# A planner's numbers are measured anew, and the low part of two weights gets all 128 rows

## The chip, the cores and the metric

The kernel runs on one core of one Trainium2 chip. The metric is the device time of one execution in microseconds (us). Before the change the median of three runs was 1872.74 us (1870.92 to 1876.2).

## The reference

One step of an encoder layer, over 1024 prompt rows and 64 sample rows. The normalised input goes through one input projection; half of its columns feed differential attention (8 heads), half feed an RWKV-7 recurrence (16 heads of 64). Both results are gated and go through one output projection. The change touches the decay and rate weights (`w_up`, `a_up`, 64 rows each) and the order in which all of it is emitted.

```python
proj = rms_norm(x, norm_pre) @ w_in
# A: attention on rotated q, k: two softmaxes per head, w = p0 - lam * p1; rms norm; silu gate
# B: RWKV-7 on the token-shifted columns
decay = exp(-exp(-softplus(-(w0 + tanh(wd) @ w_up)) - 0.5))
a = sigmoid(a0 + ad @ a_up)
kk = kb * k_k; kk = kk / max(norm(kk), 1e-12); kb = kb * (1 + (a - 1) * k_a)
for t in time:                      # per head, state s is 64 x 64
    sa = s @ (-kk_t)
    s = s * decay_t + outer(sa, kk_t * a_t) + outer(v_t, kb_t);  y_t = s @ r_t
y_b = (group_norm(y) * ln_w + ln_b + bonus) * silu(g)
out = concat(y_a, y_b) @ w_out
x + rms_norm(out, norm_post); also k, v, the last state, the last shifted row
```

## The kernel before

**Precision.** A value of 32 bits is split into a high and a low part, and a product is done as three matmuls: high by high, low by high, high by low. In the input projection that is a *triple* L215, L216, L217; eight triples fill one tile of 384, 384 or 320 columns, and three tiles make a *job*, the 128 projected columns of one head or pair of heads. The output projection has its triple at L1145, L1146, L1147, of 512 columns.

**Phase B** (L282) works on units: a pair `p` of heads (0 to 7) and a half `hf` of the prompt, 512 rows, which makes 16, and one unit for the sample, put in at the 16th place of 17. A unit first makes its vectors (decay, rate, `kk`: L490 to L620; the decay and rate weights are applied at L513 and L514, once for the high part and once for the low), then 128 x 128 blocks and the inverse of a triangular block by doubling (L630 to L790), and then runs its *chain* of eight chunks of 64 rows (L800 to L850). A chunk of the chain is: two matmuls on the state, L804 and L809; a copy L818 by VectorE; the matmul L821; two copies L827 and L828; the matmuls L832 and L833; two updates of the state L842. The next chunk needs the state. The chains of the units follow one another, while the next unit is prepared.

**Phase A** (L1164) is attention, by head and by tile of 128 queries: scores L1322 and L1323, a maximum L1332 and the sum of weights by VectorE, exponentials L1348 by ACT, transposes L1381, the product with v L1395, and the norm and gate. It starts when all units are done. Its q and k are read back from DRAM by loads that SP issues (L1206, L1207), and the cast of k is at L1249.

**Fillers.** The stream `filler` (L974) emits the projection's jobs: r, k, v and g of each pair as soon as the tiles of the pair before are free, and in between the heads' aq, ak, av, ag, of which `RESERVE = 6` are held back until the pairs are done. Its products are evacuated by ACT and VectorE (a gate's sum at L939, the rotation at L964 to L966). After the last job and the end of phase B the same stream becomes the output projection (L1040): eight groups, 0 to 3 for the RWKV half and 4 to 7 for the attention heads, each over nine tiles of rows. Groups 0 and 2 are evacuated by a copy of ACT, the others by an add of VectorE, L1156. `finish` (L1117) follows group 7.

**What sets the order.** The order is laid when the kernel is built: the order of emission is the priority by which instructions are scheduled, and on the chip each engine runs its own list in order. `Weave` holds streams (generators), sorted by rank: units by their number, fillers 100. It keeps a virtual clock `now` for PE. The first stream that may go on emits its next instructions; `spend(ns)` says how long PE is busy with them, `op(engine, n)` books an operation of n elements in that engine's queue and returns when its result is there, and `yield d` lets the stream go on d ns later. In between, a stream of lower rank emits. So the fillers stand in the gaps that the clock sees, and the numbers of the planner (latency, rate, fixed cost, which operations are booked at all) decide how many triples stand in a gap.

## Time and profile before

| | before |
|---|---|
| median of 3 runs | 1872.74 us (1870.92 to 1876.2) |
| the profiled execution | 1870.95 us |
| its span (first to last instruction) | 1869.1 us |
| mean granted clock of PE | 0.975 |
| PE busy | 1699.6 us, 91% |
| weight loads (PEld) busy | 1500.6 us, 80% |
| VectorE busy | 1305.8 us, 70% |
| ACT busy | 868.1 us, 46% |
| GpSimd (POOL) busy | 695.4 us, 37% |

PE's busy time counts a matmul from its start to its modelled end, and matmuls overlap; how long one holds up the next is read from the distance of two starts. The time that an engine is not busy in a stretch is its wait there. In a wait list, the name behind the arrow is the instruction that came last.

### The profile page before, as it was taken

How to read it: one execution, taken by the hardware profiler on the slowest of the kernel's cores; microseconds unless marked ns; L12 is line 12 of the kernel's file. 1: busy time of each engine (PE TensorE's matmuls, PEld its weight loads, DVE VectorE, ACT ScalarE, POOL GpSimd, SP SyncE). 2: the span in 40 equal slices, each digit the busy share in tenths (PEclk: the TensorE clock that was granted, in tenths of full speed). 3: DMA queues.
4: the chain of work that ended last, by engine and by line, in shares of the span. 5: the costliest groups of instructions: out<-in, count | busy, mean ns of one | idle time of the engine just before them, and what ended most of it. 6: DMA issues, size and time to landing. Idle time of an engine off the chain costs nothing. (4 is left out here: it accounts for less than half of the span.)

```text
span 1869.1 us, 34871 instructions
## 1 busy us (share of the span) xinstructions
PE 1699.6 (91%) x12930; PEld 1500.6 (80%) x12930; DVE 1305.8 (70%) x2892; ACT 868.1 (46%) x2155; POOL 695.4 (37%) x866
## 2 busy tenths in 40 slices
PE   6999899999998999999999899977899798889995
PEld 5888888888888888888888789877778676777784
DVE  5568777777778787886875766524687667787336
ACT  5534444344344444444443433323566576676323
POOL 4442333233233323323332421212332356554657
PEclk9999999999999999999999999998999899899998
DMA  4110111321122111110101121345555565443325
GB/s 144 49 55 27 50 48 48 80 82 36 39 72 62 51 44 35 52 38 29 57 26 50 57 62 50 106 118 160 153 156 149 165 155 156 121 131 105 116 87 181
DMA packets 204244, 158.85 MB, mean 85 GB/s; under 512 B 44229, under 2 KB 185194, under 8 KB 204074
## 3 DMA queue, kind: packets, MB, share of 16 engines
q1 hardware_dynamic: 169242, 137.33, 25.5%
q10 hardware_dynamic: 34832, 19.30, 4.0%
q8 instruction: 102, 1.67, 0.4%
q14 instruction: 68, 0.56, 0.1%
HBM read 108.67 MB, written 47.34 MB: 83 GB/s over the span
## 5 line engine op out<-in xcount | busy, mean ns | idle before, releaser
L1348 ACT ACTIVATE e<-s,nb 128x512 f32<-128x512 f32 (+4 forms) x208 | 117.3, 569 | 59.3 <-DVE nb L1332 26.1
L1145 PE MATMUL po<-woh,mxh 128*128 128x512 f32 x288 | 120.3, 419 | 7.1 <-DVE part L1156 5.9
L1147 PE MATMUL po<-wol,mxh 128*128 128x512 f32 x288 | 115.9, 402 | 3.9 <-DVE nb L1337 2.5
L1146 PE MATMUL po<-woh,mxl 128*128 128x512 f32 x288 | 115.5, 401 | 4.2 <-POOL mxl L158 4.2
L1332 DVE TENSOR_REDUCE nb<-s 128x1 f32<-128x512 f32 (+4 forms) x208 | 108.0, 529 | 15.9 <-PE s L1323 14.6
L158 POOL TENSOR_TENSOR mxl<-mxr,mxh 128x512 fp32r<-128x512 f32 (+1 forms) x72 | 88.3, 1231 | 74.9 <-ACT mxh L157 61.8
L811 ACT ACTIVATE sd<-suv,dc 64x64 f32<-64x64 f32 x128 | 44.4, 347 | 154.1 <-DVE suv L842 149.4
L1322 PE MATMUL s<-k,qs 128*128 128x512 f32 (+4 forms) x208 | 78.9, 385 | 22.0 <-ACT k L1249 10.0
L1395 PE MATMUL x_o<-vn,wt 128*128 128x128 f32 (+1 forms) x608 | 88.0, 289 | 10.1 <-DVE wt L1385 5.4
L1395 PEld LDWEIGHTS x_o<-vn,wt 128*128 128x128 f32 (+1 forms) x608 | 81.0, 200 | 18.5 <-issue 5.5
L1156 DVE TENSOR_TENSOR part<-po,part 128x512 f32<-128x512 f32 x72 | 49.5, 688 | 55.6 <-PE po L1147 55.5
L842 DVE SCALAR_TENSOR_TENSOR suv<-cbank,dc,sd 64x64 f32<-64x64 f32 x224 | 63.0, 281 | 33.3 <-PE cbank L832 29.2
L832 PE MATMUL cbank<-suv,bkt 128*128 128x128 f32 x256 | 56.9, 304 | 32.0 <-DVE suv L828 32.0
L832 PEld LDWEIGHTS cbank<-suv,bkt 128*128 128x128 f32 x256 | 41.1, 190 | 45.7 <-DVE suv L828 43.4
L215 PE MATMUL pj_v<-hhi,wh_v 128*128 128x384 f32 (+1 forms) x192 | 70.1, 365 | 6.5 <-DVE mg L416 6.1
L1409 POOL TENSOR_SCALAR ms<-ms 128x1 f32<-128x1 f32 x72 | 18.0, 249 | 150.9 <-ACT osq L1407 150.4
L1323 PE MATMUL s<-k,qs 128*128 128x512 f32 (+4 forms) x208 | 71.5, 358 | 2.4 <-POOL k L1252 1.5
L215 PE MATMUL pj_av<-hhi,wh_av 128*128 128x384 f32 (+1 forms) x192 | 70.2, 365 | 3.0 <-DVE fl_g L939 3.0
L157 ACT CAST mxh<-mxr 128x512 fp32r<-128x512 f32 (+1 forms) x72 | 40.7, 567 | 68.7 <-PE po L1147 29.4
L677 POOL TENSOR_TENSOR ltlo<-lt,lt 64x512 f16<-64x512 f32 x32 | 37.7, 1177 | 93.4 <-ACT lt L665 92.2
L1145 PEld LDWEIGHTS po<-woh,mxh 128*128 128x128 f32 x288 | 55.4, 192 | 20.6 <-DVE part L1156 4.4
L215 PE MATMUL pj_k<-hhi,wh_k 128*128 128x384 f32 (+1 forms) x192 | 67.7, 352 | 4.0 <-ACT raw_k L230 4.0
(533 smaller groups left out, 6189.5 us busy)
## 6 DMA issues: line engine op xcount, KB each, us to landing
mxr<-mixB SPq DMA_DIRECT2D x32, 256.0 KB
wor<-in_w_out SPq DMA_DIRECT2D x64, 128.0 KB
qa<-scr_q SPq DMA_DIRECT2D x32, 204.0 KB
ka<-scr_k SPq DMA_DIRECT2D x32, 204.0 KB
scr_q<-fl_q SPq DMA_DIRECT2D x8, 544.0 KB
scr_k<-fl_k SPq DMA_DIRECT2D x8, 544.0 KB
scr_v<-fl_v SPq DMA_DIRECT2D x8, 544.0 KB
scr_g<-fl_g SPq DMA_DIRECT2D x8, 544.0 KB
```

The source lines that it names most:

```text
L158: gtt(lo, raw, hi.bitcast(F32), op=SUB)
L215: mm(ps[:, :n], hi[:, k, :], hhi[i][:, k, :], start=(k == 0), stop=False)
L832: mm(s, bkt[:, c], suv[:, c], start=True, stop=True)
L842: stt(suv[r, c + 1, h, :] if c < 7 and not smp else to[r], s[r, h * CH:(h + 1) * CH], dc[r, c:c + 1], sd[r], op0=MUL, op1=ADD)
L1145: mm(ps, hi[:, q, :], wh, start=(q == 0), stop=False)
L1146: mm(ps, lo[:, q, :], wh, start=False, stop=False)
L1147: mm(ps, hi[:, q, :], wl, start=False, stop=(q == len(ks) - 1))
L1322: mm(s[:, 0:w], lq, k1[c][:, k0 + o_:k0 + o_ + w], start=True, stop=False)
L1323: mm(s[:, 0:w], lq, k2[c][:, k0 + o_:k0 + o_ + w], start=False, stop=True)
L1332: nc.vector.tensor_reduce(nb[:, i_:i_ + 1], s[:, 0:w], axis=AX.X, op=MAX, negate=True)
L1348: act(e[:, o_:o_ + w], s[:, 0:w], AF.Exp, bias=mx, accum_out=sm)
L1395: mm(ops[:, 0:P], wt[0:w, b, :], vn[0:w, vb, :], start=(b == 0), stop=(b == len(kbs) - 1))
```

## The change

It has two parts. The same instructions are issued by each engine in the same number; their order changes, and one operand.

**The planner.** A result is there 210 ns after PE (130 or 100 before) and 60 ns after another engine. An operation costs a rate times its elements plus a fixed part for each instruction, which was 80 ns for all and is now 150, 190 and 90 on VectorE, ACT and GpSimd. `op` takes a number of instructions `k` and an earliest start `at`. `spend` adds 130 or 105 ns where the work changes to matmuls on part of the array or back. The fillers' evacuations, shifts, gates and rotations, which were not booked, are. Many sizes of booked operations and spent times are set anew.

**The low part.** L514 multiplied 64 rows of the low part (rows 0 to 63 for `w_up`, 64 to 127 for `a_up`) by the same 64 rows of the input. Now it multiplies all 128 rows, of which the other half belongs to the low part as it lies in the tile.

```diff
-LA, LAT, W_LD, W_DMA = 130, 100, 11000, 3122
+LAT, OUT, W_LD, W_DMA = 210, 60, 11000, 3122
+LA = LAT
+
+T_IN, T_OUT = 130, 105
...
-RS = 1.0
 RATE = {DVE: 1 / 0.96, ACT: 1 / 1.2, POOL: 2.4}
+FIX = {DVE: 150, ACT: 190, POOL: 90}
...
-    def spend(self, ns):
+    def spend(self, ns, part=False):
+
+        if part != self.part:
+            self.part = part
+            ns += T_IN if part else T_OUT
         self.now += ns
...
-    def op(self, eng, n):
-
-        self.free[eng] = max(self.now, self.free.get(eng, 0.0)) + RS * (RATE[eng] * n + 80)
-        return self.free[eng] - self.now + (LA if b_done[0] else LAT)
+    def op(self, eng, n, k=1, at=0.0):
+
+
+        self.free[eng] = max(self.now + at, self.free.get(eng, 0.0)) + RATE[eng] * n + k * FIX[eng]
+        return self.free[eng] - self.now + OUT
...
             nc.scalar.copy(raw[:, 1 + t0:1 + t0 + n], ps)
+            weave.op(ACT, n, at=LAT)
...
                 act(d, raw[:, t0 + 1:t0 + 1 + n], AF.Copy, scale=omu[:, idx:idx + 1])
+                op_(DVE, n, at=op_(ACT, n + 80))
...
                         stt(d_, d_, 1.0, ps[:, a - t0:b - t0], op0=ADD, op1=MUL)
+                        op_(DVE, b - a, at=op_(ACT, b - a, at=LAT))
...
-                    for j, (x, r) in enumerate(((xw, slice(0, 64)), (xa, slice(64, 128)))):
+                    for j, x in enumerate((xw, xa)):
...
                         mm(o_, t[:, j], x[:, cl], start=True, stop=False)
-                        mm(o_, t[r, 2 + j], x[r, cl], start=False, stop=True)
+                        mm(o_, t[:, 2 + j], x[:, cl], start=False, stop=True)
...
-            op_(DVE, 4100)
+            op_(DVE, 8 * 512, 8)
...
-                spend(1800)
+                spend(1400, True)
...
-                yield done(op_(DVE, 6 * 256 + 400), 2)
+                yield done(op_(DVE, 6 * 256, 6), 2)
...
-            d = op_(DVE, 800)
+            d = op_(DVE, 1400, 3)
...
-                op_(DVE, 110)
+                op_(DVE, 128)
...
-            yield op_(DVE, 1200)
+            yield op_(DVE, 1040, 3)
...
             vtt(yo, yo, gate, op=MUL)
+            op_(DVE, 600)
...
                     stt(st_[:, t0:t0 + n], st_[:, t0:t0 + n], 1.0, ps, op0=ADD, op1=MUL)
+                    op_(DVE, n, at=op_(ACT, n, at=LAT))
...
                 vtt(a, a, b, op=ADD)
+                op_(DVE, 3 * W, 3)
...
-        op_(ACT, n)
-        return op_(POOL, n)
+        return op_(POOL, n, at=op_(ACT, n))
...
-            spend(w / 1.2 + 20)
+            spend(w / 1.1 + 10)
...
-            d = op_(ACT, w + 50)
+            d = op_(ACT, w + 80, 2)
```

The lines move by some: the chain's L804, L821, L832 are L818, L835, L846 after the change, the projection's triple is L224 to L226, the low part L526 and L527, the output projection's triple L1161 to L1163.

Three places show what the order does. The first is PE in a chunk of a chain, between L821 and L832 before. `cbank` is the chain's PSUM tile, `pj_k` a projection tile, `m_bo` a product of the next unit.

```order
L821 MATMUL cbank<-gsb_01_4937,xtf 128x128
L651 MATMUL m_bo_10_4961<-t_kbh_1_4784,bdr 128x512
L652 MATMUL m_bo_10_4961<-t_kbl_1_4785,bdr 128x512
L215 MATMUL pj_k_1_4911<-hhi_174,wh_k_4531 128x384
L216 MATMUL pj_k_1_4911<-hlo_177,wh_k_4531 128x384
L217 MATMUL pj_k_1_4911<-hhi_174,wl_k_4532 128x384
L215 MATMUL pj_k_2_4978<-hhi_175,wh_k_4531 128x320
L832 MATMUL cbank<-suv_0_4717,bkt_0_4689 128x128
L833 MATMUL y_00_4807<-suv_0_4717,rbk_0_4008 128x128
L216 MATMUL pj_k_2_4978<-hlo_178,wh_k_4531 128x320
L217 MATMUL pj_k_2_4978<-hhi_175,wl_k_4532 128x320
```

After the change, such a place between L835 and L846 of the same unit (`y_00`), with the four matmuls of the decay and rate weights (`m_up`) just ahead; `pj_av` is a projection tile. The dots stand for the rows up to the last matmul of the fourth triple.

```order
L526 MATMUL m_up_00_5379<-xw,t_wus_00_5381 128x512
L527 MATMUL m_up_00_5379<-xw,t_wus_00_5381 128x512
L526 MATMUL m_up_01_5380<-xa,t_wus_00_5381 128x512
L527 MATMUL m_up_01_5380<-xa,t_wus_00_5381 128x512
L835 MATMUL cbank<-gsb_01_5372,xtf 128x128
L224 MATMUL pj_av_0_5348<-hhi_173,wh_av_5092 128x384
L225 MATMUL pj_av_0_5348<-hlo_176,wh_av_5092 128x384
L226 MATMUL pj_av_0_5348<-hhi_173,wl_av_5093 128x384
...
L226 MATMUL pj_av_1_5411<-hhi_174,wl_av_5093 128x384
L554 MATMUL m_ss_00_5425<-on_483,t_sq_0_5395 128x2 x4
L846 MATMUL cbank<-suv_0_5109,bkt_0_5047 128x128
L847 MATMUL y_00_5194<-suv_0_5109,rbk_0_4312 128x128
```

Before, two matmuls of a unit, one triple and the first matmul of a second stand in the gap, and the triple goes on behind the chain's L833. After, four triples and a short sum of a unit stand in it, and no triple is cut; the four `m_up` rows read alike in shape.

The second place is PE in the last unit's chain. Before, it is one round of it:

```order
L804 MATMUL cbank<-suv_1_14687,pt_498 128x128
L809 MATMUL y_14_14954<-suv_1_14687,pt_498 128x128
L215 MATMUL pj_ak_0_15011<-hhi_173,wh_ak_14842 128x384
...
L217 MATMUL pj_ak_0_15011<-hhi_173,wl_ak_14843 128x384
L821 MATMUL cbank<-gsb_15_15020,xtf 128x128
L215 MATMUL pj_ak_0_15011<-hhi_173,wh_ak_14842 128x384
...
L217 MATMUL pj_ak_0_15011<-hhi_173,wl_ak_14843 128x384
L832 MATMUL cbank<-suv_1_14687,bkt_1_14656 128x128
L833 MATMUL y_14_14954<-suv_1_14687,rbk_1_14035 128x128
L215 MATMUL pj_ak_0_15011<-hhi_173,wh_ak_14842 128x384
```

After the change, a round and the start of the next:

```order
L835 MATMUL cbank<-gsb_13_16022,xtf 128x128
L846 MATMUL cbank<-suv_1_15879,bkt_1_15848 128x128
L847 MATMUL y_10_15949<-suv_1_15879,rbk_1_15188 128x128
L1161 MATMUL po_16268<-woh_16234,mxh_16218 128x512
L1162 MATMUL po_16268<-woh_16234,mxl_16219 128x512
L1163 MATMUL po_16268<-wol_16235,mxh_16218 128x512
L818 MATMUL cbank<-suv_1_15879,pt_498 128x128
L838 MATMUL y_14_16034<-suv_1_15879,pt_498 128x128
L1161 MATMUL po_16284<-woh_16234,mxh_16224 128x512
L1162 MATMUL po_16284<-woh_16234,mxl_16225 128x512
L835 MATMUL cbank<-gsb_14_16038,xtf 128x128
L1161 MATMUL po_16268<-woh_16248,mxh_16218 128x512
```

Before, two projection triples stand in each of these gaps, of tile `pj_ak`; after, no projection is left, and one to three matmuls of the output projection's first group (`po`) stand in a gap, or none.

The third place is SP's queue where attention's first loads of q (`qa`) are issued. Before:

```order
L928 DMA mixB_124<-ysq_o_1_15216 128x512
L967 DMA rot_q_163<-raq_15167 128x136
L944 DMA scr_k_141<-fl_k_15162 128x1088
L1037 DMA out_shift_p<-sho 25x128
L1037 DMA out_shift_s<-sho 25x128
L949 DMA rot_k_167<-fl_k_15162 16x1088
L950 DMA rot_k_168<-fl_k_15162 8x1088
L1206 DMA qa_15287<-rot_q_160 16x1088
L1207 DMA qa_15287<-scr_q_126 48x1088
```

After the change:

```order
L1098 DMA wor_17520<-in_w_out 128x256
L1116 DMA mxr_16407<-mixB_125 128x4x64
L1054 DMA out_shift_p<-sho 25x128
L1054 DMA out_shift_s<-sho 25x128
L942 DMA mixB_124<-ysq_o_1_16111 128x512
L1116 DMA mxr_16468<-mixB_123 128x4x128
L1116 DMA mxr_16539<-mixB_123 128x4x128
L1222 DMA qa_16162<-rot_q_160 16x1088
L1223 DMA qa_16162<-scr_q_126 48x1088
```

Before, the rotated rows of k (`rot_k`) and the stored projections (`scr_k`) of later heads are still written just ahead of the loads; after, these are gone by then, and loads of rows (`mxr`) and weights (`wor`) for the output projection stand there.

## Rows read from the trace of the kernel before

**Rows 1.** The page, part 1: each engine's busy time, share and instructions.
```profile
PE 1699.6 (91%) x12930; PEld 1500.6 (80%) x12930; DVE 1305.8 (70%) x2892; ACT 868.1 (46%) x2155; POOL 695.4 (37%) x866
```

**Rows 2.** Stretches: length, then PE, PEld, DVE, ACT, POOL busy, clock, DMA.
```profile
0.00:100.00 100.00, 78.04 (x435) 69.25 (x436) 58.29 (x92) 55.04 (x99) 48.07 (x79) 0.95 0.30 93
100.00:1250.60 1150.60, 1090.05 (x9497) 984.48 (x9495) 840.38 (x1820) 472.96 (x1078) 352.28 (x419) 0.99 0.19 54
1250.60:1270.40 19.80, 3.72 (x15) 2.70 (x14) 4.36 (x10) 6.58 (x12) 5.54 (x3) 0.58 0.94 230
1270.40:1746.00 475.60, 423.57 (x2551) 361.61 (x2550) 345.80 (x897) 294.39 (x883) 207.11 (x267) 0.96 0.52 139
1746.00:1870.00 124.00, 104.18 (x441) 82.59 (x439) 57.01 (x74) 39.10 (x85) 82.41 (x99) 0.95 0.43 135
```

**Rows 3.** Waits of PE, 100 to 1250.6: total us, times, longest us.
```profile
PE cbank L832 <- DVE suv L828: 32.0, 36, 3.2
PE cbank L821 <- DVE gsb L818: 7.7, 9, 1.8
...
PE cbank L804 <- DVE suv L842: 2.2, 2, 1.2
```

**Rows 4.** VectorE in order of time around 407 (start us, us, instruction).
```profile
406.75 1.84 DVE L670 TENSOR_TENSOR xt_a<-lt,mt 64x512 f16<-64x512 f16 x2
...
409.91 0.23 DVE L828 COPY suv<-cbank 64x64 f32<-64x64 f32 x1
```

**Rows 5.** PE in order of time around 410.
```profile
410.19 0.49 PE L832 MATMUL cbank<-suv,bkt 128*128 128x128 f32 x2 [0.79 <-DVE suv L828]
410.52 0.39 PE L833 MATMUL y<-suv,rbk 128*128 128x128 f32 x2
410.66 0.39 PE L216 MATMUL pj_k<-hlo,wh_k 128*128 128x320 f32 x1
410.89 0.31 PE L217 MATMUL pj_k<-hhi,wl_k 128*128 128x320 f32 x1
```

**Rows 6.** PE in order of time around 216, the low part.
```profile
215.36 0.30 PE L217 MATMUL pj_aq<-hhi,wl_aq 128*128 128x320 f32 x1
215.50 0.40 PE L513 MATMUL m_up<-xw,t_wus 128*128 128x512 f32 x1
215.83 0.49 PE L514 MATMUL m_up<-xw,t_wus 64*128 64x512 f32 x1
...
217.11 0.49 PE L804 MATMUL cbank<-suv,pt 128*128 128x128 f32 x2
```

**Rows 7.** PE in order of time at 1800, output projection.
```profile
1800.16 0.39 PE L1145 MATMUL po<-woh,mxh 128*128 128x512 f32 x1
1800.39 0.39 PE L1146 MATMUL po<-woh,mxl 128*128 128x512 f32 x1
```

**Rows 8.** PE in order of time at 1014, the sample unit.
```profile
1013.83 0.28 PE L513 MATMUL m_upNone<-xw,t_wusNone 128*128 128x64 f32 x1
...
1017.42 0.44 PE L215 MATMUL pj_av<-hhi,wh_av 128*128 128x384 f32 x1
```

**Rows 9.** PE in order of time, the first score of attention.
```profile
1262.67 0.47 PE L1322 MATMUL s<-k,qs 128*128 128x128 f32 x1 [10.02 <-ACT k L1249]
```

**Rows 10.** VectorE by line, 1262 to 1746: busy us, mean ns.
```profile
L1156 DVE TENSOR_TENSOR part<-po,part 128x512 f32<-128x512 f32 x17 | 11.6, 682 | 3.2 <-PE po L1147 3.1
...
L939 DVE SCALAR_TENSOR_TENSOR fl_g<-fl_g,pj_ag 128x384 f32<-128x384 f32 (+1 forms) x12 | 6.3, 526 | 5.2 <-ACT fl_g L938 5.2
...
L965 DVE TENSOR_TENSOR rbk<-rbk,rtk 128x136 f32<-128x136 f32 x8 | 3.7, 461 | 9.8 <-DMA rbk<-rot_k 6.7 <-DMA rtk<-in_c_rot 3.1
```

**Rows 11.** A stretch of attention (columns as in rows 2).
```profile
1400.00:1450.00 50.00, 48.25 (x330) 45.04 (x329) 39.14 (x111) 33.47 (x102) 15.92 (x25) 1.00 0.55 145
```

**Rows 12.** VectorE, lines L599 and L688: duration ns min/median/max.
```profile
L599 DVE TENSOR_TENSOR pt<-t_kkn,dd x32: 641/689/1766, 76.2 to 1113.4; 64x512 f32<-64x512 f32 x32
...
L688 DVE TENSOR_TENSOR q<-m_ip,mt x80: 664/691/693, 100.9 to 1164.7; 128x512 f16<-128x512 f32 x80
```

More of the change, by code (lines that the diff above doesn't have):

```diff
@@ L70, in __init__ @@
         self.free = {}
+        self.part = False
         self.count = itertools.count()
-    def spend(self, ns):
+    def spend(self, ns, part=False):
+        if part != self.part:
+            self.part = part
+            ns += T_IN if part else T_OUT
         self.now += ns
-    def op(self, eng, n):
-        self.free[eng] = max(self.now, self.free.get(eng, 0.0)) + RS * (RATE[eng] * n + 80)
-        return self.free[eng] - self.now + (LA if b_done[0] else LAT)
+    def op(self, eng, n, k=1, at=0.0):
+        self.free[eng] = max(self.now + at, self.free.get(eng, 0.0)) + RATE[eng] * n + k * FIX[eng]
+        return self.free[eng] - self.now + OUT
     def later(self, ns, call):
@@ L541, in unit @@
                 mm(pss[:, 2 * q:2 * q + 2], sq[:, q * P:(q + 1) * P], on2, start=True, stop=True)
-            spend(1100)
+            spend(900)
             yield LAT
@@ L555, in unit @@
             nc.gpsimd.memset(dd[:, :, 0:1], 1.0)
-            yield op_(DVE, 512)
+            yield op_(DVE, 1020)
             act(dd[:, :, 1:CH + 1], c3(cs), AF.Exp, scale=-C2)
@@ L618, in unit @@
                 stt(kbl, kb, hrk[:, p:p + 1], kbh.bitcast(F32), op0=MUL, op1=SUB)
-            op_(POOL, 960)
-            op_(ACT, 512)
+            if smp:
+                op_(POOL, 512)
+            op_(ACT, 600)
             yield op_(DVE, 512)
@@ L684, in unit @@
                     mm(ps[:, cl], lt16[:, c, :], x_[:, cl], start=True, stop=True)
-                spend(300)
+                spend(240)
                 yield LAT
@@ L694, in unit @@
                         mm(ps[r, cl], q_[r, cl], xt[r, cl], start=True, stop=True)
-                spend(500)
+                spend(340, True)
                 yield LAT
@@ L710, in unit @@
                     mm(ps[r, cl], xt[r, cl], id16[r, :], start=True, stop=True)
-            spend(500)
+            spend(340, True)
             yield LAT
@@ L723, in unit @@
                 mm(ps[:, cl], ltlo[:, c, :], x_[:, cl], start=False, stop=True)
-            spend(600)
+            spend(480)
             yield LAT
@@ L737, in unit @@
                     nc.tensor.transpose(ps[:, c * CH:(c + 1) * CH], src, ident[r, 64 * h:64 * h + 64])
-                spend(500)
+                spend(560, True)
                 yield LAT
@@ L765, in unit @@
                     mm(ps[r, cl], r16[r, cl], xt[r, cl], start=True, stop=True)
-            spend(500)
+            spend(340, True)
             yield LAT
@@ L852, in unit @@
                         nc.scalar.copy(ysb[64:128, 0:CH], y4[64:128, 3, CH:])
-                    op_(ACT, 400)
-                    op_(ACT, 400)
-                yield op_(DVE, 110)
+                    op_(ACT, 570, 3)
+                yield op_(DVE, 128)
             yield lambda: turn["norm"] == n
@@ L873, in unit @@
             gtt(var, var, nh[:, 0:8], op=POW)
-            yield op_(POOL, 700)
+            yield op_(POOL, 800, 2)
             vtt(c3(yc), c3(yc), bcol(var), op=MUL)
@@ L877, in unit @@
             nc.gpsimd.tensor_copy(ycp[64:128, HALF:], ycp[64:128, 0:CH])
-            z_at = weave.now + op_(POOL, 110)
+            z_at = weave.now + op_(POOL, 220)
             if smp or hf == 1:
@@ L939, in evac @@
                     stt(st_[:, t0:t0 + n], st_[:, t0:t0 + n], 1.0, ps, op0=ADD, op1=MUL)
+                    op_(DVE, n, at=op_(ACT, n, at=LAT))
                 else:
                     act(st_[:, t0:t0 + n], ps, AF.Copy, scale=0.125 if kind == "q" else 1.0)
+                    op_(ACT, n, at=LAT)
             yield from proj_cm(w, evac, f"a{kind}{h}")
@@ L1295, in prep @@
                 nc.tensor.transpose(ps[:, t * 64:(t + 1) * 64], k[0:64, t * P:(t + 1) * P], ident[0:64, 0:64])
-            spend(450)
+            spend(450, True)
             yield LA
@@ L1337, in score @@
             vtt(mx, nb[:, 0:1], nb[:, 1:2], op=ALU.min)
-            d = op_(DVE, 60)
+            d = op_(DVE, 10)
         yield d
@@ L1364, in qtile @@
             nc.vector.tensor_reduce(sm, st["sp"], axis=AX.X, op=ADD)
-            op_(DVE, 60)
+            op_(DVE, 10)
         ri = ap_.tile([P, 2], F32, tag="ri", bufs=3, name=f"ri{u}")
@@ L1370, in qtile @@
         stt(w_[:, 0:n], e1[:, 0:n], co, w_[:, 0:n], op0=MUL, op1=ADD)
-        op_(DVE, 400)
-        yield op_(DVE, n)
+        op_(DVE, 130, 2)
+        yield op_(DVE, n + 60)
         yield lambda: (h, 2) in ready
@@ L1403, in qtile @@
         act(on, ops[:, 0:P], AF.Copy, scale=ri[:, 0:1])
-        yield xdone(op_(ACT, P))
+        yield xdone(op_(ACT, 210))
         sq = ap_.tile([P, P], F32, tag="osq", name=f"osq{u}")
@@ L1407, in qtile @@
         act(sq, on, AF.Square, accum_out=ms)
-        yield op_(ACT, P)
+        yield op_(ACT, P, 2)
         gts(ms, ms, 1.0 / P, SUBLN_EPS, op0=MUL, op1=ADD)
```

4 lines of the change are left out of this document (2 added, 2 removed).

## The prediction

> **What bounds the kernel now.** I read the page's first part first. TensorE (PE) is busy for 91% of the span [rows 1], so a change in the order of emission can win only what PE waits, and what PE loses between instructions without being called idle. The second view is the table of stretches [rows 2], where the wait of a stretch is its length less PE's busy time. From 100 to 1250.6 us, in which sixteen prompt units and the sample unit of RWKV run beside the projections, PE waits 1150.6 - 1090.05 = 60.5 us. The passage to attention (1250.6 to 1270.4) holds 3.72 us of PE work in 19.8 us, a wait of 16.1. Attention (1270.4 to 1746) waits 475.6 - 423.57 = 52.0, and the tail 124.0 - 104.18 = 19.8; the first 100 us hold the other 22. The third view, the list of waits of the RWKV stretch, says who is waited for there [rows 3]: 32.0 us go to L832 waiting for the copies of L828, 7.7 to L821 and 2.2 to L804, together 41.9 us on the state chain, which is L804, a copy, L821, two copies, L832, an update, and again. The fourth view shows one such wait close up. VectorE runs a pair of mask products for 1.84 us from 406.75 and other work behind them, so the second chain copy starts only at 409.91 [rows 4]. PE has used up the fillers that were emitted for this gap and stands 0.79 us before L832 at 410.19 [rows 5].
>
> **The low part of the rate weights.** Nothing is removed in count: each prompt unit keeps four 512-column matmuls at L513 and L514 and the sample unit 32 short ones. What goes is the half-array form of L514 (64 rows). The row before them shows a step of 0.14 us between projection matmuls of 320 columns; the four then take from 215.50 to 217.11, 1.61 us [rows 6]. Four 512-column matmuls that keep the full array step by 0.23 us [rows 7], 0.91 us for four. So 0.70 us times 16 units, 11.2 us, on PE's own time and on no other engine. The 32 of the sample unit come in two runs of 16, of which one took 1013.83 to 1017.42, 3.59 us [rows 8], so 7.2 us in all. No row shows such a 64-column matmul in one form: at best the half-array switch is all of it (a gain of 7), at worst it is none. I take 4: by the nearest row, the 320-column step of 0.14, it is 32 x (0.22 - 0.14) = 2.6, and 64 columns are fewer. Sum: **-15**, bounds -11 to -18. The extra low-by-low products cost no columns.
>
> A rule speaks against this edit. The Trainium skill, "TensorEngine Tiling (Array Packing)", section Overview, says that a contraction of 64 or less can run in independent half arrays, for up to twice the throughput; by it, giving the 64-row slices up for full rows would cost something near the 0.45 us that it saves per pair, and the term would be +7 and not -11. The trace sides against it here: the two L514 of a unit work on different halves but with a full-array L513 between them, so nothing runs beside them. The sum goes by the rows.
>
> **The new emission order: fewer breaks.** By my count over the two orders, changes between the stream of projection triples (L215, L216, L217) and other matmuls fall from 1358 to 1172, so there are 93 fewer breaks. A break costs something even where PE is called busy: L216 after the chain's L833 took 0.23 us to its follower, where the same columns step by 0.14 inside the stream, a loss of 0.09, and L832 took 0.33 to L833, which took 0.14 itself [rows 5, 6], another 0.19 where the switch falls there. So a break is 0.09 to 0.28 us and 93 breaks are 8 to 26 us. I take the middle, 0.175 each: **-16**.
>
> **The new emission order: the chain's waits.** With longer latencies in the planner (210 ns and not 100, a fixed charge per instruction of 150 on VectorE and not 80) and with the fillers' own VectorE and ACT work charged, the planner puts more triples between chain steps: inside a unit 74.8 on average against 54.75, which is 3.5 a gap against 2.6. A triple of 320 columns is 3 x 0.14 = 0.43 us, so a gap gains about 0.4 us of cover, and of 103 gaps from L821 to L832 the ones with under 1.2 us of work between fall from 54 to 19. The 36 waits at L832 have a mean of 0.89 us [rows 3]; half a microsecond more of cover removes the short ones and leaves the tails of waits like the longest, 3.2. I take **-30** of the 41.9, bounds -10 to -40.
>
> **What that borrows.** The triples are a fixed stock, and 168 of them stood in attention before. All now stand before the last unit's chain, with three prices. First, six heads of fillers are held back until the last pairs are projected, and near the 14th and 15th chains (counted with the sample) the stock open to them is empty: some 17 gaps hold no triple. A bare gap costs at most the 0.79 of [rows 5], 13 us, and the units' own matmuls fill part: **+8**, bounds 3 to 15. Second, the last chain has no triple in 23 gaps, only single products of the first output group from its third round on: 23 x 0.79 = 18 at most, about 11 with those. Against it, the passage's 16.1 us (of which 10.0 are the first score's wait for the cast of k at L1249 [rows 9]) get the rest of group 0 and two tiles of group 1 beside them, but SP now issues the loads of q behind two loads of group 1. I take **+8** for both, bounds -5 to 25. Third, attention loses its cover of triples: a projection triple waits for nothing, while a product of the output projection ends in an add that VectorE must do. PE's work there becomes 423.6 - 81 (168 triples, at 0.14 for 320 columns and in proportion 0.17 for 384) - 98 (groups 0 to 3, 144 triples of 0.68 [rows 7]) + 141 (groups 1 to 6 less two tiles, 208 triples) = 386 us. At the old share of 0.89 it would take 434, with 48 of waits. I take 0.86, hence 448 and 62: **+10**, bounds -5 to +40. In the tail only group 7 is left, and the last head has no product beside it: **+9** out of bounds of 0 to 20.
>
> **The sum.** -15 - 16 - 30 + 8 + 8 + 10 + 9 = -26, so the span goes from 1869.1 to 1843. The profiled execution took 1870.95, 1.85 more than its span, and the median of the runs shown, 1872.74, is another 1.8 above it: 1843.1 + 1.85 + 1.8 = **1847**.
>
> **Rivals.**
> (A) *VectorE becomes the bound of attention; slower.* Its work there is 345.8 us [rows 2], 0.727 of the stretch. Groups 1 to 6 bring 52 adds where 17 stood, 35 x 0.682 = 24 us more; 12 gate sums (6.3 us) and 36 rotation products of about 0.42 us (0.46 for the one shown; 15 us) leave [rows 10]: 349 us. My 448 us need VectorE at 0.78. For it: PE waits most for VectorE's reductions and adds there. Against it: from 1400 to 1450 VectorE ran at 39.14 of 50, 0.78, with PE at 0.965 [rows 11]. If it can't hold more than 0.72, attention takes 484 us and the time is 1847 + 36 = 1883; it decides the sign from 0.727 downward, where attention takes 480.
> (B) *The waits go and nothing is given back.* Attention keeps 0.89 (-14), the bare gaps of the 14th, 15th and last chain are covered by units' own work (-12), and a break is worth 0.24 (-6): 1815. For it: those chains hold matmuls that my count of triples doesn't weigh. Against it: the last chain stands almost alone.
> (C) *The chain's waits move and stay.* The planner charges fixed durations, 683 ns for a 512-element VectorE product, but the product of L599 took from 641 to 1766 ns, while L688, which reads PSUM, stayed within 664 to 693 [rows 12]. A chain copy behind a stretched one is late by 1.08 us whatever the plan. If the -30 comes to nothing the time is 1877. Against it: gaps grow by 0.4 us and would hide half of such a delay.
>
> The rule on this: the Trainium skill, "SBUF — State Buffer", section Who interferes with whom, has a VectorE instruction with two SBUF inputs contend with a GpSimd instruction that reads SBUF. The trace agrees in its rows for L599 and L688. By it, one stretched product per unit would still meet the chain, 17 x 1.08 = 18 us of the 30, and the time would be 1865.
>
> **How the numbers follow.** Forecast 0.53, with its own range of 1825 to 1866 (the terms' errors, mostly the chain's waits and attention); A 0.16; B 0.17; C 0.14. Within 0.3% (5.6 us of 1872.74, about what a measurement of this kernel can tell from no change) is 1867.1 to 1878.4. Faster: 0.51 of the forecast, all of B, 0.05 of C and 0.02 of A, 0.75. Same: 0.02 + 0.06 of C + 0.03 of A, 0.11. Slower: 0.11 of A and 0.03 of C, 0.14. The range reaches from below B to just above A, 1808 to 1886, with about one in ten left out on each side.
>
> **What would show it.** Low part: the four matmuls of a unit within 1 us, no wide first gap after them. Breaks: the busy time of PE in total falls by about 31 us, from 1699.6. Chain: the waits at the three chain lines at about 12 us up to the 13th unit, with new ones in the 14th, 15th and last chain of about 20. Attention: about 448 us at a VectorE share of 0.78. The prediction is wrong if PE's busy time stays, if the chain's waits stay above 30 us, or if attention gets as long as before although it holds some 38 us less PE work.

## The result: slower by 2.6%, and the profile after

The changed kernel takes 1922.64 us (median of 4 runs, 1921.22 to 1923.88) against 1874.38 us in the same comparison, a ratio of 1.0259 (95% interval 1.0241 to 1.0278). The forecast was 1847 us, with a range up to 1886. The profiled execution has a span of 1922.0 us, 52.9 above the 1869.1 of before, and a mean granted clock of 0.955 where it was 0.975.

The first line of the changed kernel's page that matters answers to [rows 1]:

```profile
PE 1715.3 (89%) x12930; PEld 1524.6 (79%) x12930; DVE 1311.2 (68%) x2892; ACT 864.5 (45%) x2155; POOL 692.9 (36%) x866
```

PE's busy time rose by 15.7 us, although it issues the same matmuls and four of each unit became shorter. So the loss isn't only waiting. Cut at the chains of the units, the changed kernel reads as follows: from the second unit's chain to the 14th's, the chains of the 14th to the last unit, the passage to the first score, attention to its last score, and the tail (length, then busy PE, PEld, DVE, ACT, POOL, granted clock, DMA share, GB/s):

```profile
206.30:1126.10 919.80, 861.46 (x7340) 799.37 (x7339) 635.81 (x1361) 362.90 (x819) 282.76 (x334) 0.99 0.22 62
1126.10:1374.20 248.10, 218.38 (x1744) 193.76 (x1742) 159.50 (x365) 94.23 (x225) 69.21 (x78) 0.90 0.22 67
1374.20:1412.10 37.90, 28.61 (x108) 22.45 (x107) 11.32 (x16) 15.77 (x33) 16.35 (x19) 0.82 0.49 120
1412.10:1861.00 448.90, 387.93 (x2212) 315.69 (x2212) 340.64 (x867) 277.26 (x838) 208.02 (x266) 0.94 0.47 126
1861.00:1922.00 61.00, 37.86 (x151) 27.04 (x151) 38.88 (x61) 22.59 (x59) 40.08 (x57) 0.85 0.47 157
```

The same pieces of the kernel before, its first two (its whole is in [rows 2]):

```profile
195.80:977.20 781.40, 740.85 (x6547) 665.69 (x6546) 607.10 (x1311) 337.83 (x764) 252.44 (x309) 1.00 0.17 51
977.20:1222.20 245.00, 228.52 (x1895) 207.63 (x1894) 156.64 (x359) 91.56 (x216) 65.22 (x66) 0.98 0.23 66
```

In the first piece PE stands 58.3 us and not 40.6, in the second 29.7 and not 16.5, and the clock in the second is 0.90 and not 0.98. To compare orders that put different work in a piece, I split each span into three: PE's busy time as it would be at full clock (busy less half of what was busy at the granted clock of 0.5, from the trace's clock records), PE's waits, and half of the busy time at half clock. The last two are the *loss*. Taking half is a little too much: from one matmul of a projection triple of 384 columns to the next it is 0.174 us at full clock and 0.320 at half (medians over the kernel before), a factor of 1.84 and not 2, so the prices of the half clock below are some 9% too high and the work too low by as much time. Each split is read from one execution, which need not be the median one.

| one profiled execution each, us | span | work at full clock | waits | half clock's price | loss: units 2 to 13 | last chains and passage | attention |
|---|---|---|---|---|---|---|---|
| before | 1869.1 | 1667.5 | 169.6 | 32.2 | 44.0 | 33.0 | 70.0 |
| after | 1922.0 | 1646.1 | 206.7 | 69.2 | 68.4 | 65.8 | 80.5 |

The work fell by 21 us. Waits rose by 37, and the half clock costs another 37. The rest of the loss, the start and the tail, went from 54.8 to 61.2.

**Inside the units.** The waits of PE from 206.3 to 1126.1 in the changed kernel (total us, times, longest) answer to [rows 3]:

```profile
PE m_zt L919 <- ACT suv L769: 11.0, 6, 2.4
PE cbank L835 <- DVE gsb L832: 10.1, 9, 3.1
PE cbank L846 <- DVE suv L842: 9.7, 12, 2.0
PE m_iq L708 <- DVE q L702: 7.2, 8, 2.1
PE m_zt L919 <- DVE ycp L888: 5.6, 2, 4.9
PE m_ip L698 <- DVE x L717: 5.6, 3, 3.2
```

Over the whole span the chain's three lines fell from 41.9 us [rows 3] to 34.5:

```profile
PE cbank L835 <- DVE gsb L832: 15.2, 13, 3.1
PE cbank L846 <- DVE suv L842: 14.9, 19, 2.0
PE cbank L818 <- DVE suv L856: 4.4, 6, 2.0
```

In their place PE stands at the transposes of a unit's norm (L919, 30.7 us in all) and in the triangular inverse (L698 and L708, 15.9 us against 3.3). The norm's transposes before, at L906, were waited for 2.3 us:

```profile
PE m_zt0None L906 <- DVE ycp L875: 1.6, 1, 1.6
PE m_zt L906 <- DVE ycp L875: 0.7, 1, 0.7
```

One of the new waits, ACT around 815, then PE, GpSimd and VectorE:

```profile
810.68 0.31 ACT L769 COPY suv<-m_vt 64x192 f32<-64x192 f32 x1
814.83 0.72 ACT L630 ACTIVATE t_kbh<-t_kb,dv 128x512 fp32r<-128x512 f32 x1 [3.84 <-DVE t_kb L618]
815.58 0.37 ACT L767 COPY suv<-m_vt 64x256 f32<-64x256 f32 x1
815.96 0.47 ACT L769 COPY suv<-m_vt 64x256 f32<-64x256 f32 x2
```

```profile
813.67 0.60 PE L919 MATMUL m_zt<-ident,ycp 128*128 128x128 f32 x4
814.10 0.39 PE L818 MATMUL cbank<-suv,pt 128*128 128x128 f32 x2
816.38 0.66 PE L919 MATMUL m_zt<-ident,ycp 128*128 128x128 f32 x4 [1.89 <-ACT suv L769]
```

```profile
812.38 1.69 POOL L615 TENSOR_TENSOR bk<-t_kb,t_cs 64x512 f32<-64x512 f32 x1
```

```profile
814.11 0.69 DVE L618 TENSOR_TENSOR t_kb<-t_kb,mr 128x512 f32<-128x512 f32 x1 [1.18 <-POOL bk L615]
```

The second tile of `m_zt` needs a PSUM tile that ACT empties by the copies L767 and L769. They stand in ACT's list behind L630, whose input comes from VectorE's L618, which waited for GpSimd's L615. ACT stood 3.84 us with the copies behind it. The planner books L615, L618 and L630 each on its own engine's queue, and nothing tells ACT's queue that L630's input comes last.

**The clock.** The 4.9 us from 209.6 to 214.5 are the longest wait at L919; the four stretches are: ahead of it, the wait, behind it, and after that (columns as above):

```profile
204.50:209.60 5.10, 5.04 (x43) 4.59 (x41) 5.01 (x9) 3.85 (x11) 1.89 (x8) 1.00 0.18 51
209.60:214.50 4.90, 0.00 (x0) 0.01 (x1) 3.07 (x4) 2.18 (x6) 4.17 (x4) 0.97 0.00 0
214.50:217.60 3.10, 3.08 (x13) 3.10 (x14) 2.34 (x5) 1.91 (x4) 0.71 (x2) 0.50 0.29 85
217.60:222.00 4.40, 4.40 (x37) 4.03 (x36) 3.43 (x8) 0.82 (x2) 0.00 (x0) 1.00 0.16 60
```

At a granted clock of 0.50, the 1.2 GHz level, PE issued 13 matmuls in 3.1 us; in the 4.4 us at 1.00, or 2.4 GHz, 37. Such a wait is paid twice. Not every long wait is: in the changed kernel's first piece eleven are over 1.8 us, and right behind five of them (1.91 to 4.93 us) the clock fell to half, behind the other six (1.89 to 3.20 us) it did not. The kernel before has 6.8 us of half clock from the second unit's chain to the 14th's, the changed one 20.5; the last chains and the passage had 19.1 and have 61.4 (lengths of the stretches, partly idle). The Trainium skill, "TensorE: Matmul & The Clock Gate", Part 1, says that the clock is gated by PE's recent activity; the rows agree, and the prediction's sum had no term for it.

**The last chain.** PE, from the second round of the last unit:

```profile
1346.02 0.64 PE L818 MATMUL cbank<-suv,pt 128*128 128x128 f32 x2
1346.45 0.63 PE L823 MATMUL y<-suv,pt 128*128 128x128 f32 x2
1349.38 0.49 PE L835 MATMUL cbank<-gsb,xtf 128*128 128x128 f32 x2 [2.29 <-DVE gsb L832]
1351.10 0.80 PE L846 MATMUL cbank<-suv,bkt 128*128 128x128 f32 x2 [1.23 <-DVE suv L842]
1351.69 0.64 PE L847 MATMUL y<-suv,rbk 128*128 128x128 f32 x2
```

With nothing between, PE stands 2.29 and 1.23 us in one round, and L847 takes 0.64 us where L833 took 0.39 [rows 5]: the half clock again.

**The low part**, answering to [rows 6]: two of a unit's four matmuls, which now start 0.23 us apart. In fourteen of the sixteen prompt units the four together took 0.91 to 1.18 us, where those of rows 6 took 1.61.

```profile
1216.31 0.39 PE L526 MATMUL m_up<-xw,t_wus 128*128 128x512 f32 x1
1216.54 0.40 PE L527 MATMUL m_up<-xw,t_wus 128*128 128x512 f32 x1
```

### The profile page after: what moved, and what is told of

The parts are those of the page before. It is cut to its first block, busy times and chain, and to the rows that moved or that the text cites. A ratio compares the mean times of both kernels' runs of the same rounds, so it can differ in the third digit from the quotient of the medians.

```text
span 1922.0 us, 34806 instructions
## 1 busy us (share of the span) xinstructions
PE 1715.3 (89%) x12930; PEld 1524.6 (79%) x12930; DVE 1311.2 (68%) x2892; ACT 864.5 (45%) x2155; POOL 692.9 (36%) x866
## 4 chain that ended last, share of the span: by engine, by line
PE 57%; DVE 17%; POOL 8%; DMA 6%; ACT 6%; issue 5%; ACTq 1%; POOLq 0%; SPq 0%; DVEq 0%
PE x_o L1411 2%; PE po L1162 2%; PE po L1161 2%; PE po L1163 2%; PE cbank L846 2%; PE cbank L835 2%; PE pj_ak L224 1%; PE s L1338 1%; PE pj_av L224 1%; PE pj_ak L225 1%; PE pj_ak L226 1%; PE pj_k L224 1%; PE cbank L818 1%; PE pj_ag L224 1%; PE pj_aq L224 1%
## 5 line engine op out<-in xcount | busy, mean ns | idle before, releaser
L1161 PE MATMUL po<-woh,mxh 128*128 128x512 f32 x288 | 128.4, 447 | 15.1 <-DVE part L1172 7.6
L1162 PE MATMUL po<-woh,mxl 128*128 128x512 f32 x288 | 121.1, 420 | 8.8 <-POOL mxl L167 8.7
L1163 PE MATMUL po<-wol,mxh 128*128 128x512 f32 x288 | 120.7, 420 | 1.0 <-POOL wol L167 0.9
L1338 PE MATMUL s<-k,qs 128*128 128x512 f32 (+4 forms) x208 | 79.9, 390 | 24.9 <-ACT e L1364 13.5
L856 DVE SCALAR_TENSOR_TENSOR suv<-cbank,dc,sd 64x64 f32<-64x64 f32 x224 | 63.0, 281 | 36.7 <-PE cbank L846 32.2
L1161 PEld LDWEIGHTS po<-woh,mxh 128*128 128x128 f32 x288 | 58.3, 203 | 30.0 <-DVE part L1172 6.8
L702 DVE TENSOR_TENSOR q<-m_ip,mt 128x512 f16<-128x512 f32 x80 | 55.1, 689 | 28.9 <-PE m_ip L698 28.1
L224 PE MATMUL pj_k<-hhi,wh_k 128*128 128x384 f32 (+1 forms) x192 | 70.6, 368 | 4.1 <-ACT raw_k L239 4.1
L1162 PEld LDWEIGHTS po<-woh,mxl 128*128 128x128 f32 x288 | 58.3, 202 | 19.9 <-POOL mxl L167 11.7
L1338 PEld LDWEIGHTS s<-k,qs 128*128 128x128 f32 x208 | 41.5, 201 | 40.7 <-ACT e L1364 23.3
L846 PE MATMUL cbank<-suv,bkt 128*128 128x128 f32 x256 | 58.2, 310 | 15.0 <-DVE suv L842 14.9
L224 PE MATMUL pj_g<-hhi,wh_g 128*128 128x384 f32 (+1 forms) x192 | 70.7, 368 | 0.0
L224 PE MATMUL pj_av<-hhi,wh_av 128*128 128x384 f32 (+1 forms) x192 | 70.5, 367 | 0.0
```

What stands on the lines that cost most here:

```text
L224: mm(ps[:, :n], hi[:, k, :], hhi[i][:, k, :], start=(k == 0), stop=False)
L846: mm(s, bkt[:, c], suv[:, c], start=True, stop=True)
L856: stt(suv[r, c + 1, h, :] if c < 7 and not smp else to[r], s[r, h * CH:(h + 1) * CH], dc[r, c:c + 1], sd[r], op0=MUL, op1=ADD)
L1161: mm(ps, hi[:, q, :], wh, start=(q == 0), stop=False)
L1162: mm(ps, lo[:, q, :], wh, start=False, stop=False)
L1163: mm(ps, hi[:, q, :], wl, start=False, stop=(q == len(ks) - 1))
```

## The experiments

Sixteen runs in four groups. The times are medians; the ratio is to the kernel before, run beside them. The table gives the same split as above, from one profiled execution each.

| run | median, us | ratio (95%) | work | waits | half clock | units 2 to 13 | last chains | attention |
|---|---|---|---|---|---|---|---|---|
| after | 1922.64 | 1.0259 (1.0241, 1.0278) | 1646.1 | 206.7 | 69.2 | 68.4 | 65.8 | 80.5 |
| low_only | 1866.07 | 0.9951 (0.993, 0.9971) | 1654.6 | 183.7 | 26.1 | 46.5 | 36.9 | 70.5 |
| planner_only | 1935.21 | 1.0315 (1.03, 1.0331) | 1660.7 | 204.3 | 67.8 | 68.2 | 65.0 | 79.5 |
| fixed_80 | 1887.24 | 1.0069 (1.0048, 1.009) | 1655.1 | 185.6 | 39.9 | 59.5 | 28.3 | 79.9 |
| no_filler_booking | 1915.84 | 1.0201 (1.0174, 1.0227) | 1646.4 | 202.9 | 55.6 | 71.2 | 56.0 | 67.8 |
| triple_plus_200 | 1898.63 | 1.0143 (1.0101, 1.0185) | 1653.3 | 188.2 | 50.9 | 75.5 | 30.2 | 80.0 |
| norm_3us_later | 1900.99 | 1.0159 (1.0111, 1.0206) | 1643.5 | 188.3 | 70.0 | 63.0 | 60.2 | 76.8 |
| before_low_fixed | 1848.83 | 0.9873 (0.9834, 0.9913) | 1638.6 | 161.5 | 50.8 | 58.0 | 29.6 | 67.7 |
| before_low_latency | 1890.39 | 1.0093 (1.0063, 1.0123) | 1652.4 | 189.3 | 46.9 | 58.5 | 35.8 | 87.0 |
| old_latency | 1906.91 | 1.0181 (1.0165, 1.0197) | 1645.3 | 200.6 | 61.1 | 71.2 | 68.6 | 64.9 |
| before_low_booked | 1884.32 | 1.0057 (1.0039, 1.0074) | 1651.3 | 181.0 | 50.0 | 73.5 | 24.5 | 70.5 |
| kbh_after_its_inputs | 1918.75 | 1.0244 (1.0221, 1.0266) | 1648.1 | 206.2 | 58.3 | 69.7 | 57.2 | 75.3 |
| attention_as_before | 1914.76 | 1.0228 (1.0206, 1.025) | 1643.6 | 201.4 | 60.8 | 69.1 | 67.1 | 76.9 |
| charges_3_percent | 1919.42 | 1.0237 (1.0221, 1.0253) | 1647.9 | 210.9 | 58.4 | 93.3 | 33.8 | 81.8 |
| after_latency_220 | 1897.02 | 1.0114 (1.0097, 1.0131) | 1645.6 | 197.8 | 58.5 | 59.9 | 49.9 | 84.1 |
| fixed_140 | 1868.37 | 0.9967 (0.9954, 0.9981) | 1639.8 | 178.1 | 53.6 | 72.8 | 36.5 | 65.2 |
| fixed_160 | 1898.51 | 1.0127 (1.0112, 1.0142) | 1642.5 | 198.8 | 54.5 | 79.5 | 28.4 | 80.2 |

### Which part, and the pace

Before with the low part alone, and the changed kernel with the low part put back:

```diff
-                        mm(o_, t[r, 2 + j], x[r, cl], start=False, stop=True)
+                        mm(o_, t[:, 2 + j], x[:, cl], start=False, stop=True)
```

> The kernel before with the low part alone over all 128 rows. The order of emission is that of before. Theory A (pace: the order is what lost, the low part is a gain): 13 to 15 us under before, since PE's busy time at the low part's two lines fell from 33.9 to 20.9 us in the changed kernel. Rival B (the low part itself costs, for instance through a dearer load of 128 rows of weights): not under before.

> The changed kernel with the low part put back on 64 rows; the planner's numbers and the order stay as in the changed kernel. Theory A: about 13 us above the changed kernel, 1936. Rival B: 1922 or less, as the low part would give nothing or cost.

The low part is a gain: 1866.07 against 1875.94, 9.9 us, and taking it out of the changed kernel costs 12.6 (1935.21 against 1922.64). PE's work fell by 12.9. Rival B is out, and the planner's numbers alone cost 59 us. Their order was then slowed to the pace of before in two ways, by the charge of each operation and by that of each triple, and in a third run the seven bookings of fillers were taken out (one of them is shown):

```diff
-FIX = {DVE: 150, ACT: 190, POOL: 90}
+FIX = {DVE: 80, ACT: 80, POOL: 80}
...
-                weave.spend(3 * n / 2.4 + 60)
+                weave.spend(3 * n / 2.4 + 260)
...
-            weave.op(ACT, n, at=LAT)
```

> The changed kernel with the fixed cost of an operation back at 80 ns on every engine; latencies, bookings of fillers, sizes and low part stay. By count, a unit then holds about 74 triples and not 94, and 219 triples are left when the last chain begins (271 in the kernel before, none in the changed one). Theory A (pace: the larger fixed costs make a unit look longer, so the projections are used up before the last chains, which then run bare at half clock): 1845 to 1865. Rival C (queues: the new latencies and bookings place instructions so that PE stands at the transposes of the norm and in the inverse): 1900 or more, as those are unchanged.

> The changed kernel with 200 ns added to what the planner spends for each projection triple; its charges for all other engines stay. By count a unit then holds about 70 triples and 302 are left when the last chain begins, as in the kernel before. Theory A (pace: what loses is that the projections are used up, whatever number does it): 1850 to 1880, half-clock busy time back near 60 us from 138. Rival C (queues: the new charges place the units' own instructions so that PE stands at them): above 1895, with the waits at the transposes of the norm (L919) and the inverse still 30 us or more.

> The changed kernel without the seven bookings of fillers' ACT and VectorE operations; fixed costs and latencies stay. By count, a unit then holds about 84 triples, the 14th and 15th chains are covered (81 and 98) and 56 are left for the last. Theory A: the bare chains go, which are 31 us of waits and half clock in the units from the 14th; 1880 to 1895. Rival C: within 10 us of the changed kernel if latencies and fixed costs misplace the unit's own instructions.

Both ways of slowing give the last chains their triples back, and the loss there falls from 65.8 us to 28.3 and 30.2. That part of theory A is shown. By the traces the loss of the last chains goes with the triples left for the last one throughout: 24 to 37 us in every run with 126 or more, 56 with 56, and 50 to 69 with none. But theory A's times are missed: 1887 lies between its range and rival C's, and 1899, against at most 1880, is what rival C expected, with 30.0 us of waits left at the norm's transposes alone. With 302 triples left, where the kernel before has 271, triple_plus_200 still loses 75.5 us inside the units. There the waits at the norm's transposes are the largest (PE, 195 to 994):

```profile
PE m_zt L919 <- DVE ycp L888: 20.0, 9, 4.5
PE cbank L846 <- DVE suv L842: 15.5, 14, 2.8
```

So pace is one loss and not the whole. Without the bookings, the last chain still had only 56 triples and the passage to attention stood 20.7 us. Its 1916 us miss theory A, and are within the 10 us of the changed kernel that rival C allowed; inside the units the loss didn't fall (71.2 us against 68.4).

### Single waits taken away

```diff
-            z_at = weave.now + op_(POOL, 220)
+            z_at = weave.now + op_(POOL, 220) + 3000
```

> The changed kernel with the transposes of the norm (L919) told to wait 3000 ns more; pace by count unchanged (94 triples a unit, none left for the last chain). In the changed kernel PE stood 31 us at L919 in all. Theory A: those waits go, the bare last chains stay; 5 to 20 us under the changed kernel, 1902 to 1917. Rival C (the waits at L919 and the half clock behind them are the main loss): 30 us or more under, 1892 or less.

```diff
-            op_(DVE, 8 * 512, 8)
+            yield op_(DVE, 8 * 512, 8)
```

> The changed kernel, in which a unit's stream waits for VectorE's booked queue before it emits the ACT operation L630, so that L630 should not stand at the head of ACT's queue before its input is there; the pace by count stays (94 a unit, none left for the last chain). In the changed kernel PE stood 13 us at L919 for ACT's copies of m_vt, which stood behind L630. Theory F (a blocked head of ACT's queue makes these waits): they go, 8 to 25 us under the changed kernel with the half clock behind them. Otherwise: within 6 us.

The first took 1901, 1 us under theory A's range and 9 above rival C's; the second 1919, within 6 us of the changed kernel, so theory F's gain was missed. Yet the waits that each aimed at shrank. PE's waits at these lines over the span, in norm_3us_later and then in kbh_after_its_inputs:

```profile
PE cbank L846 <- DVE suv L842: 28.0, 26, 4.2
PE cbank L835 <- DVE gsb L832: 16.5, 15, 2.3
PE m_zt L919 <- DVE ycp L888: 11.9, 3, 4.4
```

```profile
PE cbank L846 <- DVE suv L842: 29.8, 26, 2.5
PE m_zt L919 <- ACT suv L769: 2.6, 2, 1.3
PE m_zt L919 <- ACT suvNone L769: 2.2, 1, 2.2
```

In the first, all waits at L919 fell from 30.7 to 13.6 us. In the second, those for ACT's copies fell from 13.1 to 4.8, but the edit didn't do what it was to do: ACT still stood 37.2 us in all ahead of its 16 L630 (39.6 in the changed kernel), and such a place could still hold up PE. ACT and PE at 746:

```profile
746.05 0.72 ACT L630 ACTIVATE t_kbh<-t_kb,dv 128x512 fp32r<-128x512 f32 x1 [4.47 <-DVE t_kb L618]
747.60 1.07 PE L919 MATMUL m_zt<-ident,ycp 128*128 128x128 f32 x4 [4.18 <-DVE t_kbl L631]
```

So that a blocked head of ACT's list makes these waits is read from the trace, as at 815 us, and not shown by this run. L846 went from 14.9 to 28.0 and to 29.8. A wait that is cured by moving one instruction came back at another, in an order in which the later places had moved as well.

### One set of numbers at a time

Three of the planner's changes alone, on before with the low part (fixed costs, latencies, bookings, of which one line is shown), and two undone in the changed kernel: the latencies, last in the diff, and all of attention's numbers, whose code from the end of phase B on is then that of before:

```diff
-        self.free[eng] = max(self.now, self.free.get(eng, 0.0)) + RS * (RATE[eng] * n + 80)
+        self.free[eng] = max(self.now, self.free.get(eng, 0.0)) + RATE[eng] * n + FIX[eng]
...
-LA, LAT, W_LD, W_DMA = 130, 100, 11000, 3122
+LA, LAT, W_LD, W_DMA = 210, 210, 11000, 3122
-        return self.free[eng] - self.now + (LA if b_done[0] else LAT)
+        return self.free[eng] - self.now + 60
...
+            weave.op(ACT, n)
...
-LAT, OUT, W_LD, W_DMA = 210, 60, 11000, 3122
-LA = LAT
+LAT, OUT, W_LD, W_DMA = 100, 60, 11000, 3122
+LA = 130
```

> The kernel before with the low part, and of the planner's change only the fixed costs of 150, 190 and 90 ns; latencies, sizes and unbooked fillers as before. By count 78 triples a unit, 166 left for the last chain (271 before). Theory A: a third of the way from 1866 to the changed kernel, 1875 to 1890. Rival C (latencies and bookings do it): within 6 us of 1866.

> The kernel before with the low part, and of the planner's change only the latencies: 210 ns after PE and 60 ns after another engine; operations cost as before. By count 72 triples a unit, 302 left for the last chain. Theory A: no slower than the low part alone, 1855 to 1870. Rival C: 1880 or more.

> The kernel before with the low part, and of the planner's change only the bookings of the fillers' evacuations, shifts, gates and rotations, at the rates and fixed cost of before. By count 75 triples a unit, 227 left for the last chain. Theory D: the bookings move filler work away from the chain's copies and take nothing from the last chain; 1850 to 1868. Rival E': the bookings misplace as the latencies do; 1880 or more.

> The changed kernel with the planner's latencies of before (100 ns after PE, 130 in attention; 60 after another engine stays); fixed costs, bookings, sizes stay. By count the pace is that of the changed kernel (94 triples a unit, 55 and 63 at the 14th and 15th chain, none for the last). Theory D (two separate losses: bare last chains, about 33 us in waits and half clock, and the longer latencies' placement inside the units, about 20): the bare chains stay, the units' loss falls; 1900 to 1912. Theory A (bare chains alone): within 6 us of the changed kernel, 1922. Rival E (the latencies are the whole loss, as they made 24 us on the kernel before): 1880 or less.

> The changed kernel with the planner's numbers of before in attention and from the end of phase B on (latency 130, fixed 80, sizes and spent times of before, no charge for part tiles); up to there the order is word for word that of the changed kernel. Theory D: attention's waits and half clock (61 us and 39 of half clock, against 60 and 20 with the low part alone) come from its fewer fillers and not from its numbers; within 8 us of the changed kernel. Rival G (attention's new numbers cost): 12 us or more under it.

The fixed costs alone make the kernel faster, 1848.83, the best of all: ratio 0.9873, and 17 us under the low part alone. Theory A expected 1875 to 1890. The same fixed costs cost 35 us in the changed kernel (1922.64 less 1887.24), where each instruction of a booked operation is charged and not the operation once. The latencies alone cost 24 us and the bookings alone 18 over the low part; undoing the latencies in the changed kernel gave 16 back, inside theory D's range, and attention's numbers 8, at the edge of it. The first met its range by luck: theory D looked for the gain inside the units, whose loss rose from 68.4 to 71.2 us, and it came in attention, 80.5 to 64.9. Of the 24 us that the latencies alone cost, too, 16.5 are loss in attention. These pieces don't add up: -17, +24 and +18 make 25 of the 57 us between low_only and the changed kernel, and one of them has another sign by itself than it has in company. The rest of the numbers (the sizes, the spent times, the charge where the work changes to part of the array) were not tried alone, so how much of the other 32 us is theirs stays open. By what was expected of each run, before_low_latency met rival C and not theory A, and before_low_booked met rival E' and not theory D; rivals E and G are out by their numbers.

### How smooth is the time in the planner's numbers?

```diff
-RS = 1.0
+RS = 1.03
...
-LAT, OUT, W_LD, W_DMA = 210, 60, 11000, 3122
+LAT, OUT, W_LD, W_DMA = 220, 60, 11000, 3122
...
-FIX = {DVE: 150, ACT: 190, POOL: 90}
+FIX = {DVE: 140, ACT: 180, POOL: 90}
```

(and 160, 200 and 90 in fixed_160)

> The kernel before with the low part and all charges of engine operations 3% higher; by count 262 triples left for the last chain (271). Theory S (each order has waits of its own, and the numbers of before were fitted to one): 10 us or more from the low part's 1866, more likely above. Theory N (a particular number misplaces): 1860 to 1871.

> The changed kernel with 220 ns after PE in place of 210; by count 72 and 94 triples at the 14th and 15th chain (55 and 63), still none for the last. Theory S: 10 us or more from the changed kernel's 1922. Theory N: the bare gaps of those two chains are fewer, so 1910 to 1920.

> The version before_low_fixed with fixed costs of 140, 180 and 90 ns in place of 150, 190 and 90. Theory S: 10 us or more from its 1849, more likely above. Theory N: 1843 to 1855.

> The version before_low_fixed with fixed costs of 160, 200 and 90 ns; by count 126 triples are left for the last chain. Theory S: 10 us or more from 1849, more likely above. Theory N: 1843 to 1857.

Theory S holds in all four. Charges that are 3% higher, with no other edit, cost 53 us (1866.07 to 1919.42), nearly the 57 of all the planner's changes. 10 ns more of latency give 26 us back. 10 ns less or more of fixed cost on the fastest version cost 20 and 50. In charges_3_percent 262 triples are left for the last chain, and the last chains lose 33.8 us, as before; nearly all of the loss is inside the units, from 46.5 to 93.3. Its PE there (length 826.8, busy 755.64, clock 0.97) and low_only's over the same units (776.2, 729.71, clock 1.00):

```profile
196.80:1023.60 826.80, 755.64 (x6592) 690.12 (x6592) 616.15 (x1321) 338.71 (x771) 251.65 (x317) 0.97 0.17 48
```

```profile
194.30:970.50 776.20, 729.71 (x6546) 662.67 (x6545) 607.22 (x1311) 337.12 (x764) 251.94 (x309) 1.00 0.18 51
```

46 more matmuls can't explain 50.6 us; 24.7 are waits, 22 the half clock. And the waits are at the lines that the changed kernel has too (PE, 206 to 1010, the lines L832, L906 and L684 being the changed kernel's L846, L919 and L698):

```profile
PE cbank L832 <- DVE suv L828: 28.0, 24, 4.6
PE m_zt L906 <- ACT suv L755: 8.9, 3, 3.0
PE m_zt L906 <- DVE ycp L875: 8.3, 4, 3.2
PE m_ip L684 <- DVE x L703: 4.6, 6, 1.0
```

So such waits come without any of the change's numbers. Each order has its own, and some of the long ones bring the half clock.

## Why the prediction was wrong

**The low part** (-15, bounds -11 to -18) was right in mechanism and near in size: work -12.9 us, time -9.9 and -12.6. The rule of the Trainium skill, "TensorEngine Tiling (Array Packing)", Overview, weighed against it in the prediction, would have made it a loss; the rows stood.

**Fewer breaks** (-16, bounds -8 to -26) came out at half: PE's work at full clock fell by 8.5 between low_only and the changed kernel (1654.6 to 1646.1), at the lower bound; that the fewer breaks made this isn't shown, as no run changes them alone. (The middle of 0.09 and 0.28 is also 0.185 and not 0.175, a term of 17.) PE's busy time, the sign that I named, rose: I had not seen that busy time is a sum of work and clock.

**The chain's waits** (-30, bounds -10 to -40) is the step that failed. I took the waits of one order at three lines and asked how far longer gaps would cover them, as if the rest of the order stood still. The chain's waits fell by 7.4 us to 34.5, above the 30 that I had named as the sign of being wrong, and new ones of 28 us at the norm's transposes and 13 in the inverse came, in an order in which every in-order queue had been dealt anew. With its half clock the loss from the second unit's chain to the 14th's rose by 24 us where the term had it fall by 30: 54 of the 79 us by which the span was missed. The prediction had no term for waits that are not in the trace of before. Its rival C, "the chain's waits move and stay", was the right idea with too small a price: it let the 30 us come to nothing and no further.

**The clock** has no term in the sum at all. The rows showed 0.58 in the passage [rows 2], and I priced bare gaps at their waits alone. It costs 37 us more than before, as much as the added waits.

**What that borrows.** The bare gaps were seen in the order and put at +16 (8 + 8, bounds up to 40 together). They cost 33 (33.0 to 65.8), of which 11 are waits and 22 the half clock. The mechanism is shown by fixed_80 and triple_plus_200, the term was mis-sized by the clock.

**Attention** was forecast at 448 us for a stretch that took 475.6 before [rows 2], at a VectorE share of 0.78. From its first to its last score, which is another stretch, it took 448.9 with 340.64 us of VectorE, 0.76. The same stretch of before:

```profile
1262.70:1726.00 463.30, 408.62 (x2473) 349.73 (x2474) 336.78 (x877) 289.27 (x863) 200.46 (x252) 0.95 0.54 146
```

So that 448.9 is near 448 is luck. What compares is the term: the loss rose by 10.5 us against the +10, of which 4.2 are the half clock that the term didn't hold. Rival A isn't what happened, though the sign was its. One of its reasons was misread as well: from 1270.4 to 1746 PE waited 2.5 us for VectorE's maximum, and most for the sum of weights and for copies. The tail's +9 was +3.

**The range** was built from the errors of the terms. The four small shifts show what it should have held: the same edit in kind, by a few per cent, moves the time by 20 to 53 us, and three of the four made it slower. A change that lays the whole order anew is then much like a draw. The 57 us between low_only and the changed kernel come with this order, as the instructions are the same: its loss is larger by 29 us at the last chains, 22 inside the units and 10 in attention. That the new numbers are worse than the old isn't shown. Whether measured durations help on average stays open: of fifteen orders here that are not before's, one is faster than low_only's and one within 3 us of it. That before's numbers were chosen by trial would fit, but no run shows it. Why particular instructions meet in one order and not in the other was followed for single waits only, as at 815 us.

## What to carry to other kernels

Where a planner lays the order of in-order engines, measure how far the time moves when one of its numbers is shifted by a few per cent, before you ask what a better number gives; here that spread is larger than any term of the sum. Price a wait with the clock that may follow it: here a few long waits on TensorE cost more than many short ones of about the same sum (the last section has the two runs). Keep the edits that shorten work whatever the order (the low part, 10 to 13 us) apart from those that deal the order anew, and time several of the latter; the best found here, before with the low part and the fixed costs, takes 1848.83 us, 1.3% under the kernel before.

## What the hardware showed that I had not expected

In low_only 46.5 us of waits from the second unit's chain to the 14th's, two of them over 2 us and the longest 3.1, came with no busy time at the granted clock of 0.5. In before_low_fixed 45.8 us of waits over the same units, seven of them over 2 us and the longest 5.4, came with 24.5 us of it, and in the changed kernel 58.3 us, seven over 2 us and the longest 4.9, with 20.2. And the same product on VectorE, L888, took 0.69 us in the example at 811 and 1.74 at 212.6 while GpSimd was at work, which agrees with the prediction's reading of L599 [rows 12]. It isn't so each time that GpSimd works beside it: VectorE's L616, a product over 512 elements, took 0.69 us at 812.24 although GpSimd's L615 began at 812.38.
